# A two-block kernel: the mixers of block 1 with the tensor engine in the order of the plan

## The chip, the cores and the metric

The kernel runs on one NeuronCore of one Trainium2 chip. The metric is the device time of one execution in microseconds (us); less is better. All times below are of executions of the whole program, from its first to its last instruction on that core.

## The reference, cut to what matters

Two blocks follow each other. Block 1 has three mixers on 512 tokens (a gated convolution, a neighbourhood attention, and a gated delta net with 4 heads in two directions), an output projection and a mixture of experts; block 2 comes behind it and isn't touched. Of block 1 the part that matters here is the scan of the delta net: a state is carried from chunk to chunk, and each step needs the state of the one before it.

```python
def _gated_delta_chunked(q, k, v, g, beta):     # once forward, once on flipped inputs
    ...
    sol = lax.linalg.triangular_solve(lower, rhs, left_side=True, lower=True, unit_diagonal=True)
    ...
    def step(state, xs):
        u_c, w_c, intra_c, q_c, k_c, gl_c = xs
        v_new = u_c - jnp.einsum('bhcd,bhde->bhce', w_c, state)
        o_c = jnp.einsum('bhcd,bhde->bhce', q_c, state) + jnp.einsum('bhcs,bhse->bhce', intra_c, v_new)
        state = state * jnp.exp(gl_c)[..., None, None] + jnp.einsum('bhcd,bhce->bhde', k_c, v_new)
        return state, o_c
    _, o = lax.scan(step, s0, xs)
```

The kernel takes chunks of 128 tokens, so a scan has 4 steps.

## The kernel before

The front of block 1 (norm, the first projections, the attention tables) is written in a fixed order. Behind it comes the stage of the change, the **plan**: from about 77 us to about 395 us of the span it runs everything that the mixers need.

The plan (class `Plan`, `run` at L116) is a list of Python generators with priorities. Each `yield cost, delay` tells the plan what the piece just written costs and how long the generator wants to wait before its next piece. `run` takes, at each turn, the first generator by priority whose wait is over. So the order in which instructions are *traced* is made by costs and delays written as constants. Six kinds of generators take part:

- `head(h)` for each of the 4 heads of the delta net: `prep` (decay matrices; a triangular inverse of 16 rows on GpSimd, tiles `Xb`, `Xt`, `XbT`, sent through DRAM by SyncE as `xd` and read back as `X`, `XT`), then `levels` (inverse up to 128 rows: `XT,G`, `X,BT`), then `scan`, then `norm`.
- `kqv` (L714, L737): a convolution's result `cv` or a normalised tile `nat`, transposed by the tensor engine.
- `na_all`: the attention.
- `dense` (lowest priority): the projections `hT,wh` / `hT,wl`, 128x512 matmuls, three per step of 128 input columns, yielded one such step at a time. The weights come as 1 MB tiles `ws` (a pool of 3), are rounded by ScalarE to `wh`, and the rest `wl = ws - wh` is made by VectorE or GpSimd. These matmuls fill the tensor engine's time between the pieces of the heads. `dense` also issues the `adascr` sums of the modulation (VectorE).

The **scan** (L954 to L1018) uses, per step and direction, one PSUM bank `b` in four quarters:

```python
                    mm(q_[0], kq[:, h, c, 0, :], S[d], True, True)             # -> R (DVE)
                mm(q_[1], Y[d][:, c], rhs, True, True)                          # -> vw (ACT)
                    ts_(kd, kn[h][:, c], ekd[:, d, c, h:h + 1], 0.0, OP.mult, OP.add, nc.gpsimd)
                    mm(q_[3], kd, vw, True, True)
                    if step == 0:
                        nc.scalar.copy(Sn, q_[3])                               # L994
                    else:
                        stt(Sn, S[d], egl[:, d, c, h:h + 1], q_[3], OP.mult, OP.add)
                if step:
                    mm(q_[2], kq[:, h, c, 1, :], S[d], True, True)
                mm(q_[0], C["I"][d][:, c], vw, True, True)
```

In the profile `mm` is L186, `stt` L189, `tt` L192, `ts_` L198; the matmul of `q_[3]` is `b<-vw,kd`, that of `q_[2]` is `b<-S,big`, the second one of `q_[0]` is `b<-vw,dec`. A 128x128 matmul in full float32 stands in the trace as two records, a 128x512 one of rounded values as one. Semaphore waits are set between instructions that touch the same tile, and for PSUM the tile is the bank `b`: a matmul into a bank waits for an earlier read of that bank. The read of the new state `Sn` and the matmul into `q_[2]` (at step 0: `q_[0]`) are in one bank.

What each engine then executes is not the traced order. A scheduler of the framework takes the traced instructions and may move them on each engine, as long as data is kept. `in_order` (L210) is the kernel's tool against that: it adds, between one instruction and the next of the engines named, an edge that says "behind this one", without a semaphore. Around the plan it is set for SyncE with `chain=False` (L1107), which keeps the DMA issues of the plan behind those of the front and leaves their order open. The stages behind the plan (output projection, experts, block 2) have their own `in_order` and don't depend on it.

Of the kernel before, what the change touches and what calls it, by code (L numbers as in the profile page):

```python
# [147 lines left out]
def kernel(ctx: ExitStack, tc: tile.TileContext, a: dict, out, dbg=None, stop=99):  # L148
# [56 lines left out]
    def order(i, before):  # L205
        tc.add_manual_dep(i, before.name, mybir.DependencyInfo(mybir.DependencyClass.NoSync, mybir.DependencyReason.DATA),
                          reason="order of issue")

    @contextmanager
    def in_order(chain=True, ENG=ENG):  # L210


        traced = nc.cur_bb.bb.instructions
        last = traced[-1]
        yield
        n = next(k for k in reversed(range(len(traced))) if traced[k] is last) + 1
        prev = {}
        for i in reversed(traced[:n]):
            if i.engine in ENG and i.engine not in prev:
                prev[i.engine] = i  # L220
                if len(prev) == len(ENG):
                    break
        for i in traced[n:]:
            if i.engine in ENG:
                if i.engine in prev:
                    order(i, prev[i.engine])
                if chain:
                    prev[i.engine] = i
# [400 lines left out]
    plan = Plan()  # L629
# [406 lines left out]
    def head(h):  # L1036
        if h > 1:
            yield from need("L%d" % (h - 2))
        yield from prep(h)
        if h > 1:  # L1040
            yield from need("S%d" % (h - 2))
        yield from levels(h)
        yield from scan(h)
        yield from norm(h)
# [12 lines left out]
    def dense():  # L1057
        nat_out()
        for m, (t, x, y) in enumerate(TILES):
            if m < 2:  # L1060
                o = pt0[m]
                if m == 1:
                    nxt_w = slab_tile(2)
            else:
                wl_ = nxt_w
                nxt_w = slab_tile(m + 1) if m + 1 < len(TILES) else None
                o = bank()
                yield from proj_T_steps(o, *wl_, hT, KT)
            plan.done("m%d" % m)
            if m == 2:  # L1070
                zero_scratch()
                decay()
                plan.done("decay", 3.0)
            if m > 2:
                ada_step(1)
            if m > 1:
                ada_load()
            if m == ADX:
                ada_load()
            if m == ADX + 1:  # L1080
                ada_step()
            if m == len(TILES) - 2:
                st["wo"] = wtile(a["w_outT"][0])
            if m == len(TILES) - 1:
                wo_ahead.extend(csplit(st["wo"][:, i], [P, KT, P]) for i in range(2))
            if t == "n":
                post_nqk(x, o)
            elif t == "c":
                post_conv(x, y, o)
            elif t == "z":  # L1090
                zs[x] = ht("zs")
                silu2(zs[x], o, zs[x])
                plan.done("z%d" % x, L_R)
            elif t == "g":
                plan.add(PK, kqv(x, y, o))
        while ada_left or ada_next:
            ada_step()
            ada_load()
        ada_bias(mods2, "bada2", 0, 16)

    def na_all():
        yield from need("m%d" % ORD.rindex("n"))
        yield 0.0, 2.0
        for _ in na_units():
            yield 1.5, L_NA

    with in_order(False, (mybir.EngineType.SP,)):  # L1107
        for h in range(4):
            plan.add(PH[h], head(h))
        plan.add(PN, na_all())  # L1110
        plan.add(PD, dense())
        plan.run()
    f2.close()
    front.close()
    if stop <= 1:
# [1388 lines left out]
```

## Time and profile before

| | |
|---|---|
| time, median of 3 runs (lowest to highest) | 1798.37 us (1794.47 to 1801.24) |
| the profiled execution: its time | 1804.13 us |
| its span, and mean granted clock of the tensor engine | 1802.3 us, 0.951 |
| busy in the span: PE, PEld, DVE, ACT, POOL | 1637.4, 1133.8, 946.3, 641.4, 459.9 us |

PE is TensorE's matmuls, PEld its weight loads, DVE is VectorE, ACT ScalarE, POOL GpSimd, SP SyncE (it issues the DMAs). The tensor engine is busy for 91% of the span. Times in rows are us from the span's start. In a timeline row with "x4" four neighbouring instructions of one kind stand together. A note in square brackets at the end of a row is the idle time of the engine ahead of it and what ended that.

### The profile page before, as it was taken

The page shows a single profiled execution, that of the slowest core. Times are in us where ns is not written, and L with a number is a line of the kernel's source. Part 1 is how long each engine was busy: PE and PEld are TensorE (multiplying, and loading weights), DVE is VectorE, ACT ScalarE, POOL GpSimd, SP SyncE. Part 2 cuts the span into 40 slices and gives each one's busy share as a digit, 9 for nine tenths or more (in the row PEclk, how much of TensorE's full clock was granted, in tenths as well). Part 3 has the DMA queues.
Part 4 walks back from the last instruction along what each step waited for, and adds up shares of the span by engine and source line. Part 5 has one row for each costly group of instructions (what it writes and reads, how often), then busy time and mean ns, then how long its engine had stood idle before and what let it go on. Part 6 is the DMA issues. An engine that isn't in the chain of part 4 may idle for free. (4 is left out here: it accounts for less than half of the span.)

```text
span 1802.3 us, 21878 instructions
## 1 busy us (share of the span) xinstructions
PE 1637.4 (91%) x7938; PEld 1133.8 (63%) x7938; DVE 946.3 (53%) x1832; ACT 641.4 (36%) x1293; POOL 459.9 (26%) x451
## 2 busy tenths in 40 slices
PE   4878989989689989999886889999999899999998
PEld 2767866767333334343332877776888788888886
DVE  6875777773432222222127698665437765335545
ACT  3453563432211100011112646665523554324432
POOL 5364425102100000001110422233115122332251
PEclk7889999999799989999998899999999999999999
DMA  7636244357799999999994574422313232232221
GB/s 282 216 119 201 87 154 154 129 206 293 287 396 421 419 419 421 420 418 418 418 418 175 200 262 160 163 64 78 117 71 129 82 140 88 88 111 100 88 88 47
DMA packets 97213, 385.10 MB, mean 214 GB/s; under 512 B 22624, under 2 KB 46160, under 8 KB 56656
## 3 DMA queue, kind: packets, MB, share of 16 engines
q1 hardware_dynamic: 91120, 371.09, 54.4%
q0 software_dynamic: 5984, 12.59, 1.8%
q8 instruction: 63, 1.03, 0.2%
q14 instruction: 46, 0.38, 0.1%
HBM read 372.61 MB, written 20.47 MB: 218 GB/s over the span
## 5 line engine op out<-in xcount | busy, mean ns | idle before, releaser
L192 POOL TENSOR_TENSOR wl<-ws,wh 128x1024 fp32r<-128x1024 f32 (+1 forms) x60 | 143.4, 2391 | 384.6 <-ACT wh L342 382.4
L186 PE MATMUL b<-ws,xs 128*64 128x512 f32 (+1 forms) x720 | 222.5, 625 | 11.2 <-DMA ws<-in_ew_dram 10.2
L342 ACT CAST wh<-ws 128x1024 fp32r<-128x1024 f32 (+1 forms) x154 | 152.0, 993 | 219.1 <-PE b L186 174.6
L186 PE MATMUL b<-hF,wh 128*128 128x512 f32 x656 | 202.2, 389 | 0.0
L192 DVE TENSOR_TENSOR wl<-ws,wh 128x1024 fp32r<-128x1024 f32 (+1 forms) x94 | 116.2, 1241 | 92.5 <-ACT wh L342 89.4
L186 PE MATMUL b<-hB,wh 128*128 128x512 f32 x512 | 164.3, 401 | 0.0
L189 DVE SCALAR_TENSOR_TENSOR adascr<-ws,crow 128x1024 bf16<-128x1024 f32 x96 | 135.9, 1415 | 8.2 <-DMA ws<-in_wada_dram 7.2
L186 PEld LDWEIGHTS b<-hF,wh 128*128 128x128 f32 x656 | 123.1, 188 | 25.3
L186 PEld LDWEIGHTS b<-ws,xs 128*64 128x64 f32 (+1 forms) x720 | 67.8, 146 | 109.0 <-issue 90.0
L186 PE MATMUL b<-hT,wh 128*128 128x512 f32 x384 | 132.5, 423 | 0.0
L186 PE MATMUL b<-hF,wl 128*128 128x512 f32 x328 | 127.6, 389 | 0.0
L186 PEld LDWEIGHTS b<-hB,wh 128*128 128x128 f32 x512 | 96.3, 191 | 24.7 <-issue 3.2
L189 DVE SCALAR_TENSOR_TENSOR u<-b,cols,u 128x511 f32<-128x511 f32 x88 | 65.8, 748 | 79.6 <-ACT u L2327 78.0
L186 PE MATMUL b<-ws,gT 128*64 128x512 f32 (+1 forms) x376 | 97.6, 607 | 4.3 <-ACT gT L1466 3.6
L192 DVE TENSOR_TENSOR ge<-sil,b 64x512 f32<-64x512 f32 (+1 forms) x32 | 22.1, 690 | 150.6 <-ACT sil L1459 87.1
L186 PE MATMUL b<-hB,wl 128*128 128x512 f32 x256 | 101.1, 395 | 0.0
L186 PE MATMUL b<-wh,gf 128*128 128x512 f32 x288 | 88.6, 389 | 0.0
L186 PE MATMUL b<-hT,wl 128*128 128x512 f32 x192 | 79.5, 414 | 6.7 <-POOL wl L192 4.4
L186 PEld LDWEIGHTS b<-hT,wh 128*128 128x128 f32 x384 | 71.5, 198 | 14.5 <-issue 2.8
L1320 ACT ACTIVATE xs<-b,mods,ab 128x256 f32<-128x256 f32 (+1 forms) x44 | 22.8, 524 | 158.6 <-PE b L186 157.9
L186 PE MATMUL b<-we,xs 128*64 128x512 f32 (+1 forms) x232 | 76.3, 612 | 2.0 <-DMA we<-in_ew_dram 2.0
L186 PEld LDWEIGHTS b<-dg,xg 128*128 128x128 f32 x272 | 39.3, 211 | 60.5 <-issue 57.8
(486 smaller groups left out, 3207.8 us busy)
## 6 DMA issues: line engine op xcount, KB each, us to landing
ws<-in_ew_dram SPq DMA_DIRECT2D x137, 1024.0 KB, 20.8
ws<-in_wada_dram SPq DMA_DIRECT2D x48, 1024.0 KB, 4.9
we<-in_ew_dram SPq DMA_DIRECT2D x40, 1024.0 KB, 20.7
ws<-in_w_upT_dram SPq DMA_DIRECT2D x22, 1024.0 KB, 4.9
ws<-in_w_in2T_dram SPq DMA_DIRECT2D x16, 1024.0 KB, 7.8
kg<-in_ew_dram SPq DMA_DIRECT2D x14, 1024.0 KB, 16.8
ws<-in_w_inT_dram SPq DMA_DIRECT2D x12, 1024.0 KB, 4.9
ws<-in_w_downN_dram SPq DMA_DIRECT2D x8, 1024.0 KB
```

The lines of the kernel that those rows point to most:

```text
L186: nc.tensor.matmul(o, l, r, start=start, stop=stop)
L189: return nc.vector.scalar_tensor_tensor(o, i0, s, i1, op0=op0, op1=op1, **kw)
L192: (eng or nc.vector).tensor_tensor(o, i0, i1, op)
L342: nc.scalar.copy(hi, src)
L1320: nc.scalar.activation(o, b, AF.Identity, scale=A, bias=B)
```

## The change

The plan's run stands in one more context: `in_order(True, (PE,))`. With `chain=True` each instruction of the tensor engine that the plan traces gets an edge behind the one traced before it, so TensorE takes the plan's matmuls strictly in the order in which the plan wrote them. Nothing else is edited; the order on the other engines is still the scheduler's, which now sees other times.

```diff
         plan.add(PN, na_all())
         plan.add(PD, dense())
-        plan.run()
+        with in_order(True, (mybir.EngineType.PE,)):
+            plan.run()
     f2.close()
```

Outside the plan the order of every engine stays as it was (line numbers go up by one). Within it the tensor engine, and through the scheduler the other engines, get another order. Three places:

On the tensor engine, in the scan of head 2, step 1 (`vw,kd` is `q_[3]`, `S,big` is `q_[2]`, `vw,dec` is `q_[0]`; bank `b_2489` is the forward, `b_2493` the backward direction, `b_2449` a projection):

```order
 L186 MATMUL b_2489<-vw_2517,kd_2528 128x128
+L186 MATMUL b_2489<-S_2472,big 128x128
+L186 MATMUL b_2489<-vw_2517,dec_1596 128x128
 L186 MATMUL b_2493<-vw_2520,kd_2537 128x128
+L186 MATMUL b_2493<-S_2479,big 128x128
+L186 MATMUL b_2493<-vw_2520,dec_1694 128x128
 L186 MATMUL b_2449<-hT_116,wh_2132 128x512
 L186 MATMUL b_2449<-hT_117,wh_2132 128x512
-L186 MATMUL b_2489<-S_2472,big 128x128
-L186 MATMUL b_2489<-vw_2517,dec_1596 128x128
-L186 MATMUL b_2493<-S_2479,big 128x128
-L186 MATMUL b_2493<-vw_2520,dec_1694 128x128
```

Before, the other direction's matmul and two projection matmuls stood between the `vw,kd` of a bank and the next matmul into that bank; now nothing does. The plan has 24 such pairs (4 heads, steps 0 to 2, 2 directions), and in the new order the matmul behind `vw,kd` goes into the same bank in all 24; before, 2 to 14 matmuls lay between.

On GpSimd, in the same step of head 2 (`kd` is the factor of the `vw,kd` matmuls above; `Xt`, `Xb` are the row steps of head 3's triangular inverse, `XbT` the copy at its end):

```order
 L192 TENSOR_TENSOR Xb_2312<-Xb_2312,Xt_2313 64x5x11
-L198 TENSOR_SCALAR kd_2528<-nat_1150,ekd 128x128
 L192 TENSOR_TENSOR Xt_2313<-U_2311,Xb_2312 64x48
-L198 TENSOR_SCALAR kd_2537<-nat_1150,ekd 128x128
 L192 TENSOR_TENSOR Xb_2312<-Xb_2312,Xt_2313 64x4x12
 L192 TENSOR_TENSOR Xt_2313<-U_2311,Xb_2312 64x39
```

```order
 L192 TENSOR_TENSOR Xb_2312<-Xb_2312,Xt_2313 64x15
 L901 COPY XbT_2405<-Xb_2312 64x256
+L198 TENSOR_SCALAR kd_2528<-nat_1150,ekd 128x128
+L198 TENSOR_SCALAR kd_2537<-nat_1150,ekd 128x128
 L198 TENSOR_SCALAR kd_2626<-nat_1150,ekd 128x128
 L198 TENSOR_SCALAR kd_2635<-nat_1150,ekd 128x128
```

Both `kd` move from the middle of the row steps to behind the chain and its copy.

On SyncE, where the inverse of head 0 is read back from DRAM (`X`, `XT`, 4 loads) beside the streamed 1 MB weight tiles `ws`:

```order
 L182 DMA ws_1184<-in_wada_dram 128x2048
+L182 DMA ws_1188<-in_w_inT_dram 128x2048
 L915 DMA X_1160<-xd_503 128x4x128
 L915 DMA X_1162<-xd_503 128x4x128
 L915 DMA XT_1164<-xd_504 128x4x128
 L915 DMA XT_1166<-xd_504 128x4x128
-L182 DMA ws_1188<-in_w_inT_dram 128x2048
 L904 DMA xd_505<-Xb_985 64x16x16
```

One weight tile of 1 MB is now issued ahead of the four loads instead of behind them.

## Rows read from the trace of the kernel before

**Rows 1.** Cores: span and mean granted clock.

```profile
core 0: 1802.3 us, clock 0.951
```

**Rows 2.** Windows: from:to length, busy by engine, PEclk, DMA share, GB/s.

```profile
77.00:150.00 73.00, 58.09 (x260) 45.91 (x260) 49.43 (x78) 38.42 (x94) 44.85 (x65) 0.86 0.49 152
150.00:395.00 245.00, 227.28 (x1328) 182.60 (x1327) 180.59 (x363) 113.65 (x279) 76.78 (x123) 0.98 0.44 147
480.00:930.00 450.00, 415.82 (x1912) 165.02 (x1908) 111.81 (x270) 50.06 (x99) 41.25 (x41) 0.96 1.01 415
...
129.90:136.75 6.85, 4.58 (x13) 3.39 (x12) 6.82 (x10) 4.12 (x11) 6.15 (x11) 0.50 0.00 0
```

**Rows 3.** Waits of PE, 60 to 450 us: total, times, longest.

```profile
PE b L714 <- DVE cv L189: 7.9, 4, 2.4
...
PE b L186 <- POOL kd L198: 2.0, 4, 1.2
```

**Rows 4.** Timeline, end of the plan: PE, then SP's expert loads.

```profile
397.41 0.79 PE L186 MATMUL b<-yA,wh 128*128 128x512 f32 x1 [3.52 <-DVE yA L192]
...
411.00 2.34 SPq L182 DMA_DIRECT2D ws<-in_ew_dram  x5
```

**Rows 5.** Timeline, head 0, scan step 1 (start, length, engine, instruction).

```profile
188.38 0.61 PE L186 MATMUL b<-vw,kd 128*128 128x128 f32 x4
...
188.80 0.61 DVE L189 SCALAR_TENSOR_TENSOR S<-S,egl,b 128x128 f32<-128x128 f32 x2 [2.15 <-PE b L186]
188.82 0.49 PE L944 MATMUL b<-ident,X 128*128 128x128 f32 x3
...
189.20 0.49 PE L186 MATMUL b<-S,big 128*128 128x128 f32 x2
```

**Rows 6.** Groups by line and form, 150 to 395 us: reads of the state.

```profile
L189 DVE SCALAR_TENSOR_TENSOR S<-S,egl,b 128x128 f32<-128x128 f32 x16 | 5.0, 341 | 4.7 <-PE b L186 4.7
...
L994 ACT COPY S<-b 128x128 f32<-128x128 f32 x8 | 1.8, 266 | 0.3 <-PE b L186 0.2
```

**Rows 7.** Timeline of POOL, then of PE: `kd` of head 2, step 1.

```profile
291.20 0.36 POOL L198 TENSOR_SCALAR kd<-nat,ekd 128x128 f32<-128x128 f32 x1
...
295.34 0.64 POOL L901 COPY XbT<-Xb 64x256 f32<-64x256 f32 x1
...
291.62 0.49 PE L186 MATMUL b<-vw,kd 128*128 128x128 f32 x2 [0.22 <-POOL kd L198]
```

**Rows 8.** Timeline of SP, then of PE: loads of head 0.

```profile
146.28 1.37 SPq L915 DMA_DIRECT2D XT<-xd  x2
147.71 2.05 SPq L182 DMA_DIRECT2D ws<-in_w_inT_dram  x1
...
152.72 1.13 PE L186 MATMUL b<-XT,G 128*128 128x128 f32 x8 [0.43 <-DMA XT<-xd]
```

**Rows 9.** Timeline of PE, 129 to 145 us: waits of the early stage.

```profile
129.71 0.90 PE L714 MATMUL b<-ident,cv 128*128 128x128 f32 x4 [1.71 <-DVE cv L189]
...
133.31 0.79 PE L186 MATMUL b<-hT,wl 128*128 128x512 f32 x1 [2.27 <-DVE wl L192]
...
144.85 0.79 PE L186 MATMUL b<-hT,wl 128*128 128x512 f32 x1 [4.41 <-POOL wl L192]
```

**Rows 10.** Timeline of PE, head 1: two late inputs and what follows.

```profile
206.50 0.68 PE L186 MATMUL b<-vw,kd 128*128 128x128 f32 x4 [1.86 <-ACT vw L983]
...
220.82 0.49 PE L186 MATMUL b<-vw,kd 128*128 128x128 f32 x2 [1.17 <-POOL kd L198]
...
223.14 1.05 PE L186 MATMUL b<-hT,wh 128*128 128x512 f32 x2
...
227.66 0.63 PE L186 MATMUL b<-hT,wh 128*128 128x512 f32 x2
```

**Rows 11.** Windows behind these two waits (columns as in rows 2).

```profile
222.10:225.50 3.40, 3.40 (x12) 2.90 (x12) 0.41 (x2) 1.73 (x2) 2.63 (x10) 0.50 0.00 0
...
206.50:210.00 3.50, 3.50 (x21) 2.99 (x22) 3.50 (x8) 2.45 (x7) 2.29 (x3) 1.00 0.44 118
```

## The prediction

> **What bounds the kernel now.** I began with the core's span and granted clock [rows 1] and the windows [rows 2]. From 480 to 930 us the DMA engines are full (share 1.01, 415 GB/s); before that stage and behind it the tensor engine (PE) has most of the time. In the plan's stage PE is busy for 227.28 of the 245 us from 150 to 395, while VectorE (DVE) has 180.59, ScalarE 113.65 and GpSimd 76.78: PE sets the pace there, and at most 245 - 227.28 = 17.7 us of its waits could ever be won. From 77 to 150 us it is busy for 58.09 of 73, so waits of other engines weigh more there, up to 14.9 us.
>
> Next the list of PE's waits, and single waits in the timeline [rows 3, 9, 10]: they are few and singly known (the convolution's `cv` 7.9 us in 4 waits, `kd` 2.0 in 4). What the list doesn't show is the scan: its 24 reads of the new state cost PE nothing visible now, since other matmuls stand between.
>
> Last, does a delay in the plan reach the end? Behind the plan's last projection PE waits 3.52 us for `yA` of DVE, then the output projection runs, and the expert weights begin to load at 411.00, behind the routing that follows it [rows 4]. The full DMA stage thus starts later by whatever the plan ends later, and nothing behind it has a fixed clock time. A delay passes one to one, less what that 3.52 us takes up. The span of 1802.3 is 1.8 below the execution's own 1804.13; the median of the runs is 1798.4, so I add the sum to 1804.1 for the profile and to 1798.4 for the forecast.
>
> **The change part by part.**
>
> *The 24 state reads.* Take head 0, step 1 [rows 5]. The four `vw,kd` records begin at 188.38 and the next group at 188.82, so PE spends 0.22 us on one direction. DVE starts the two reads at 188.80; one lasts 0.34 [rows 6], so the first ends at 189.14, and `S,big`, which waits for it through the bank, begins at 189.20. Meanwhile PE did the other direction's `vw,kd` and three `ident,X`. In the new order the matmul into the same bank stands directly behind `vw,kd`: from 188.38 to 189.20 is 0.82 us, of which 0.22 is work, so 0.60 is idle. The plan has 24 such pairs: 24 x 0.60 = **14.4 us**. From below: were only the read itself exposed, 16 x 0.341 (DVE) and 8 x 0.266 (ScalarE) [rows 6] would be 7.6. I take 14.4, since the start-up times are in the same row.
>
> *Reads that come late.* 0.60 holds for a reader that is idle; a single read now holds up everything on PE. DVE is busy 180.59 of 245 us with 363 instructions [rows 2], so a read meets another instruction with chance 0.74, of which on average half of 0.50 us is left: 0.18. For ScalarE, 113.65 of 245 with 279: 0.46 x 0.20 = 0.09. 16 x 0.18 + 8 x 0.09 = **3.6 us**. Bounds: nothing (the reads are moved forward by the scheduler), and a whole instruction each, 16 x 0.50 + 8 x 0.41 = 11.
>
> *`kd` of head 2, step 1.* GpSimd now makes both behind the chain of head 3 and its `XbT` copy. That copy starts at 295.34 and takes 0.64; without the two `kd` in it (0.36 each) it ends at about 295.3, and the first `kd` (0.36) is ready near 295.7, where PE began its `vw,kd` at 291.62 [rows 7]: 4.1 us late. PE itself comes later by the two round trips of step 0, 1.2 us, which GpSimd's chain doesn't wait for. In strict order nothing can be taken ahead of the waiting matmul: projections and every other head stand behind it. **2.9 us**, between 0 (PE already later by more) and 4.1.
>
> *`X` and `XT` of head 0.* Their four loads now stand behind a 1 MB weight tile in SyncE's queue. PE already waits 0.43 for `XT` [rows 8]. 1 MB at the 415 GB/s of [rows 2] is **2.5 us**. Below: 0, if the tile goes out earlier than the loads could have. Above: the tile was issued at 147.71 and `XT` at 146.28 [rows 8]; if the tile waits for a free buffer until then, the issue is late too, by at most 1.4 and its own issue, about 4.3 in all.
>
> *`kd` of head 1, step 2.* These go ahead in GpSimd's order. [...] **-2.8 us**, between 0 and -2.8.
>
> *77 to 150 us.* Here the strict order puts transposes of `cv` and `nat` ahead of projection matmuls that filled time for them, and takes other waits away: DVE's 1.71 (`cv`) and 2.27 (`wl`). But the last wait of the stretch is 4.41 for GpSimd's `wl`, ending at 144.85 [rows 9]. PE may lose or gain some 4.4 us ahead of it and go on at 144.85 all the same. Net **0**: down to -4.4 if GpSimd is earlier, up to about 3 if added waits run past that slack.
>
> *What is taken up again.* Every other engine has the same work as before and more time, so PE finds some of its other inputs ready. Half of the 3.52 for `yA` [rows 4] is 1.8; of the 7.9 for `cv` [rows 3], the longest 2.4 and the 1.71 lie before 150 us, so half of the remaining 3.8 is 1.9. **-3.7 us**, from 0 to -7.3.
>
> *Clock.* One new wait of more than 2 us (`XT`) may bring another stretch at half clock: **+1.6 us**; the new `kd` wait falls in for the one of head 1, whose stretch I took off above, so another **+1.6**. Bounds 0 and six of them, 9.6.
>
> Sum: 14.4 + 3.6 + 2.9 + 2.5 - 2.8 + 0 - 3.7 + 3.2 = 20.1. The terms overlap: PE that is late by one wait meets the next one less late. For that I take off a tenth, to **+18 us**: 1816 as a median, 1822 for a profiled execution.
>
> **The rivals.**
>
> *Absorbed, no change.* PE is only delayed where it bounds. If the delays of the scan used up the idle time that PE has anyway, all 17.7 us of it from 150 to 395 [rows 2] would cover the 18, and the time would be 1798 + 0 to 3, say 1800. For it: most waits there are on engines whose work doesn't grow. Against: much of that idle time lies at places ahead of the scans, and inputs like `cv` are made from PE's own results, which move with it.
>
> *Faster.* From 129.7 to 144.9 PE waits 1.71 + 2.27 + 4.41 = 8.4 us [rows 9]. If in the new order GpSimd makes that `wl` ahead of its chain, all of it goes, and with it the 2.8 of head 1: -11.2. It decides only where the scan costs no more than its reads, 7.6, and other terms nothing: 1798 - 11.2 + 7.6 = 1795; for a measurable gain half the reads must be hidden as well, 1791. For it: these are the longest waits of the stage. Against: GpSimd's order there is set by the chain of head 1, and the new order moves more work in front of it.
>
> *Worse: the pauses bring down the clock.* Each of the 12 scan steps now pauses PE twice by 0.60, 1.2 us in a few microseconds; a single wait of 1.17 came ahead of 3.4 us at half clock, while one of 1.86 at 206.50 was followed by the full clock [rows 10, 11]. If each step cost one such stretch, 12 x 1.6 = 19 would come instead of the 3.2: 1816 + 16 = 1832. Half of the rows speak for it, so one step in several, not each, is what I expect at most. [...]
>
> *The tensor engine reorders for itself*, so that the edges mean little: nothing in the rows shows a matmul that overtook a waiting one; at 206.50 and 220.82 all of PE stood still [rows 10]. [...] I give this rival nothing.
>
> **How the numbers follow.** The forecast, between +9 and +28: 0.63. Absorbed, within 9 us of before: 0.18. Faster by more: 0.07. Worse, +28 and up: 0.12. 0.5% is 9 us, about what a measurement of this kernel can tell from no change: slower 0.63 + 0.12 = 0.75, same 0.18, faster 0.07. The likeliest case's own range is 1807 to 1826. Its low end is the reads alone with `kd` and `XT` (7.6 + 2.9 + 2.5 - 3.7 = 9.3); its high end has the late reads at 11 (20.1 + 7.4 = 27.5). The 80% range reaches down into the absorbed case, to 1800, and up to 1832, the clock's rival; it leaves out faster (0.07), the lower half of the absorbed case (0.07) and the tail above (0.06).
>
> **What would show it.** In the changed profile: each `vw,kd` in the scans followed by a gap of about 0.6 us with DVE `S` or ScalarE `S` as its releaser, a new line in PE's waits of some 14 to 18 us in about 24 waits; PE's busy time from 150 on unchanged, its idle time up by about 18; `vw,kd` of head 2, step 1 waiting 3 us on GpSimd; `XT,G` of head 0 waiting nearly 3 us on a DMA; the first expert load near 411 + 18 = 429; the stage from 480 on the same, only shifted. The prediction fails if the gaps behind `vw,kd` are there but other waits shrink as much, if the expert loads don't shift with the plan, or if DVE's and GpSimd's new orders make inputs late or early in places that I took for equal, above all before 150 us.

## The result and the profile after

| | before | after |
|---|---|---|
| median (lowest to highest) | 1799.28 us (1794.47 to 1801.24, 4 runs) | 1832.51 us (1827.58 to 1833.22, 4 runs) |
| profiled execution: span, mean clock | 1802.3 us, 0.951 | 1830.5 us, 0.951 |

The ratio is 1.0179 with a 95% interval of [1.0164, 1.0194]: the change makes the kernel 32 us slower (1799.3 x 0.0179 = 32.2). The forecast was 18 us slower, 1816, with 1832 as the upper end of its range: the sign is right, the size is about 14 us short. On the forecast's own base it is 1798.4 x 1.0179 = 1830.6, just inside that range. All differences "in us" below are ratios times 1799.3; one ratio is uncertain by about 2 to 4 us, a difference of two by up to 5.

First the windows of the changed kernel, with the columns of [rows 2].

```profile
77.00:150.00 73.00, 52.50 (x239) 41.02 (x237) 46.78 (x75) 35.74 (x90) 40.60 (x56) 0.89 0.43 133
150.00:395.00 245.00, 211.71 (x1216) 172.13 (x1217) 164.03 (x326) 102.17 (x255) 75.36 (x131) 0.95 0.41 137
...
480.00:960.00 480.00, 428.93 (x2003) 176.12 (x2003) 129.10 (x358) 59.19 (x119) 47.76 (x55) 0.95 0.99 403
```

From 150 to 395 us PE is busy for 211.71 us where it was 227.28 [rows 2], and it did 1216 matmul records there instead of 1328: the same work isn't finished by then. The granted clock of that stretch is 0.95 instead of 0.98. From 480 us on the DMA engines are nearly as full as before (share 0.99 against 1.01). Next the list of PE's waits from 60 to 470 us (engine, line, releaser: total, times, longest).

```profile
PE b L186 <- DVE S L189: 12.5, 16, 3.5
PE b L186 <- POOL wl L192: 8.1, 1, 8.1
PE b L714 <- DVE cv L189: 7.5, 4, 2.9
PE b L737 <- DVE nat L192: 5.4, 4, 2.9
PE b L186 <- ACT S L994: 4.0, 8, 1.5
PE b L186 <- DMA XT<-xd: 3.5, 1, 3.5
PE b L186 <- DVE yA L192: 3.3, 2, 2.7
PE b L1027 <- DVE oN L192: 2.8, 2, 1.7
```

Two lines are new, the reads of the state: 16 on DVE and 8 on ScalarE, 16.5 us in all. Before, the list had no such line. GpSimd's `wl` grew from 4.41 [rows 9] to 8.1, `XT` from 0.43 in that place [rows 8] to 3.5. GpSimd's `kd` isn't there any more.

This is the step that [rows 5] show, in the timeline of the changed kernel (head 0, scan step 1):

```profile
197.73 0.39 PE L186 MATMUL b<-vw,kd 128*128 128x128 f32 x2
198.16 0.35 DVE L189 SCALAR_TENSOR_TENSOR S<-S,egl,b 128x128 f32<-128x128 f32 x1 [2.15 <-PE b L186]
...
198.56 0.49 PE L186 MATMUL b<-S,big 128*128 128x128 f32 x2 [0.44 <-DVE S L189]
198.89 0.39 PE L186 MATMUL b<-vw,dec 128*128 128x128 f32 x2
199.11 0.39 PE L186 MATMUL b<-vw,kd 128*128 128x128 f32 x2
...
199.94 0.49 PE L186 MATMUL b<-S,big 128*128 128x128 f32 x2 [0.44 <-DVE S L189]
```

From `vw,kd` to `S,big` it is 0.83 us in both directions (197.73 to 198.56, 199.11 to 199.94), as worked out from before (0.82). The profile calls 0.44 of it idle: it gives `vw,kd` 0.39 us, where PE spent 0.22 on one direction before it went on [rows 5], 0.17 less.

Where the time went, by the start of the same matmul in both traces: +5.5 us at the matmul that waits for GpSimd's `wl` (150.39 against 144.85), +8.0 at head 0's first `XT,G` (160.73 against 152.72), and about +30 at the plan's end. The plan's last wait and the first expert loads moved with it:

```profile
150.39 0.80 PE L186 MATMUL b<-hT,wl 128*128 128x512 f32 x1 [8.09 <-POOL wl L192]
160.73 1.29 PE L186 MATMUL b<-XT,G 128*128 128x128 f32 x8 [3.49 <-DMA XT<-xd]
...
426.87 0.50 PE L186 MATMUL b<-yA,wh 128*128 128x512 f32 x1 [2.69 <-DVE yA L192]
...
442.03 2.57 SPq L182 DMA_DIRECT2D ws<-in_ew_dram  x5
```

The first expert load goes out at 442.03 instead of 411.00 [rows 4], 31 us later. The two profiled spans differ by 28.2 us and the ratio gives 32.2, so within the spread of the runs what the plan loses reaches the end.

Why is GpSimd's `wl` later? These are rows of GpSimd's timeline after: four masks `dec` of head 1, which before stood in the middle of head 0's chain, now stand among its first steps, and the first of them waits for ScalarE.

```profile
113.65 2.50 POOL L192 TENSOR_TENSOR gm<-cm,g 128x512 f32<-128x512 f32 x2
119.47 1.51 POOL L192 TENSOR_TENSOR dec<-dec,cm 128x512 f32<-128x512 f32 x1 [3.32 <-ACT dec L882]
120.94 0.27 POOL L192 TENSOR_TENSOR Xt<-U,Xb 64x15 f32<-64x15 f32 x1
121.17 1.29 POOL L192 TENSOR_TENSOR dec<-dec,qk 128x512 f32<-128x512 f32 x1
...
142.45 0.60 POOL L901 COPY XbT<-Xb 64x256 f32<-64x256 f32 x1
...
148.00 2.33 POOL L192 TENSOR_TENSOR wl<-ws,wh 128x1024 fp32r<-128x1024 f32 x1
```

And the same places before:

```profile
115.10 0.21 POOL L192 TENSOR_TENSOR Xt<-U,Xb 64x15 f32<-64x15 f32 x1 [1.34 <-DMA U<-gd]
...
124.71 1.29 POOL L192 TENSOR_TENSOR dec<-dec,cm 128x512 f32<-128x512 f32 x1
...
136.89 0.63 POOL L901 COPY XbT<-Xb 64x256 f32<-64x256 f32 x1
...
142.46 2.33 POOL L192 TENSOR_TENSOR wl<-ws,wh 128x1024 fp32r<-128x1024 f32 x1
```

The chain begins 5.8 us later (120.94 against 115.10), its copy ends 5.5 later, and `wl` comes 5.5 later. Of the 5.8, the mask ahead of the chain and the wait for its input make 4.8; the rest is a later `gm`, less a shorter wait for the chain's own input.

### The profile page after: what moved, and what is told of

Same layout as the page of the kernel before. It is cut to its first block, busy times and chain, and to the rows that moved or that the text cites. A ratio compares the mean times of both kernels' runs of the same rounds, so it can differ in the third digit from the quotient of the medians.

```text
span 1830.5 us, 21867 instructions
## 1 busy us (share of the span) xinstructions
PE 1641.3 (90%) x7938; PEld 1138.8 (62%) x7938; DVE 949.1 (52%) x1832; ACT 638.7 (35%) x1291; POOL 458.5 (25%) x451
## 4 chain that ended last, share of the span: by engine, by line
PE 47%; DMA 11%; issue 6%; DVE 3%; POOL 2%; ACT 2%; DVEq 0%; POOLq 0%; SPq 0%; ACTq 0%
PE b L186 42%; DMA ws<-in_ew_dram 9%; DMA xg<-ud,gi 2%; PE b L2053 1%; PE b L1877 1%; PE b L1953 1%; DVE big L189 1%; ACT wh L342 1%; POOL wl L192 1%; PE b L2041 1%; PE b L1465 0%; DMA we<-in_ew_dram 0%; PE b L2247 0%; POOL big L192 0%; POOL hF L192 0%
## 5 line engine op out<-in xcount | busy, mean ns | idle before, releaser
L186 PE MATMUL b<-ws,xs 128*64 128x512 f32 (+1 forms) x720 | 223.0, 629 | 12.8 <-DMA ws<-in_ew_dram 12.8
```

The costliest lines, as they stand in the source:

```text
L186: nc.tensor.matmul(o, l, r, start=start, stop=stop)
```

## The experiments

The theory after the result: the strict order costs (a) the unfilled state reads, (b) a later GpSimd chain through the order of the masks, (c) later loads of `X` and `XT`, and (d) a price of its own, since late inputs of any kind are no longer filled. Rivals: the loss is (d) alone, whatever is repaired; or the clock.

| kernel | median us | ratio to before, 95% | us over before |
|---|---|---|---|
| changed | 1832.51 | 1.0179 [1.0164, 1.0194] | 32.2 |
| e1, writes first | 1819.35 | 1.0108 [1.0088, 1.0127] | 19.4 |
| e2, free order, writes first | 1801.07 | 1.0002 [0.9987, 1.0017] | 0.4 |
| e3, strict to the first scan | 1807.45 | 1.0050 [1.0031, 1.0069] | 9.0 |
| e4, strict from the first scan | 1823.11 | 1.0119 [1.0095, 1.0144] | 21.4 |
| e5, masks | 1820.65 | 1.0129 [1.0107, 1.0151] | 23.2 |
| e6, loads | 1828.34 | 1.0158 [1.0137, 1.0180] | 28.4 |
| e7, all three | 1812.90 | 1.0076 [1.0054, 1.0098] | 13.7 |
| e8, free order, masks | 1800.31 | 1.0010 [0.9998, 1.0022] | 1.8 |
| e9, states first | 1818.99 | 1.0104 [1.0086, 1.0121] | 18.7 |
| e10, writes first and masks | 1809.26 | 1.0049 [1.0033, 1.0065] | 8.8 |
| e11, scans free | 1814.35 | 1.0086 [1.0067, 1.0104] | 15.5 |
| e12, strict to the first scan, masks | 1799.53 | 0.9991 [0.9980, 1.0003] | -1.6 |

**e1, e2: the bank's writes ahead of its reads.** In each scan step all matmuls into the bank come first, so none waits for the read of the state. e1 has the strict order, e2 the free one.

```diff
-                    mm(q_[3], kd, vw, True, True)
-                    Sn = ...
                 if step:
                     mm(q_[2], kq[:, h, c, 1, :], S[d], True, True)
                 mm(q_[0], C["I"][d][:, c], vw, True, True)
+                if step < 3:
+                    mm(q_[3], kd, vw, True, True)
+                    Sn = ...
```

> Strict order as in the changed kernel, but each scan step traces its matmuls into the bank in the order q2, q0, q3 and all reads of the bank behind them, so that no matmul waits for the read of the new state. If the 24 state reads are the main price (16.5 us of waits in the changed profile, and their half-clock stretch), the time falls by 15 to 20 us against the changed kernel, to 1812 to 1817, and the waits on S shrink to under 3 us. Rival, any strict order costs the same because the matmuls that filled gaps are fixed elsewhere: within 5 us of the changed kernel, 1827 to 1833, with other waits in their place.

> The kernel before (free order) with the same new order in the scan step. If the scheduler already hid the state reads, there is nothing to win: within 4 us of before, perhaps up to 3 slower since the state is ready 0.44 us later per step. Rival, the reads cost something before too: 5 us or more faster than before.

e1 is 12.8 us under the changed kernel, e2 the same as before. The state reads cost 12.8 us under strict order and nothing under the free one, where other matmuls stood between. That is 2 us short of what was expected of e1: waits of the next step took a part over (PE's waits in e1; the changed kernel has 1.1 for `R`), and head 1's `XT` from DRAM, for which the changed kernel doesn't wait, costs 2.8.

```profile
PE b L186 <- DVE R L189: 3.8, 2, 3.1
PE b L186 <- DVE S L189: 3.1, 2, 2.8
```

The 3.1 for `R` (head 3, step 1) is a read that came late behind other work in DVE's queue (timeline of e1):

```profile
368.01 2.42 POOL L192 TENSOR_TENSOR wl<-ws,wh 128x1024 fp32r<-128x1024 f32 x1
368.17 3.35 DVE L189 SCALAR_TENSOR_TENSOR adascr<-ws,crow 128x1024 bf16<-128x1024 f32 x1
...
372.05 1.21 DVE L189 SCALAR_TENSOR_TENSOR adascr<-ws,crow 128x1024 bf16<-128x1024 f32 x1
...
373.86 0.34 DVE L189 SCALAR_TENSOR_TENSOR R<-b,neg,vn 128x128 f32<-128x128 f32 x1
...
374.25 0.79 PE L186 MATMUL b<-R,X 128*128 128x128 f32 x2 [3.08 <-DVE R L189]
```

**e9: both states first.** Both `vw,kd` and both reads stand ahead of all `q_[2]` and `q_[0]`, in two loops over the directions, so the waits are there but half filled.

```diff
             for (d, c, q_, _), vw in zip(W, V):
                 if step < 3:
                     ...
                     mm(q_[3], kd, vw, True, True)
                     ...
+            for (d, c, q_, _), vw in zip(W, V):
                 if step:
                     mm(q_[2], kq[:, h, c, 1, :], S[d], True, True)
```

> Strict order, with each scan step tracing both directions' vw,kd matmuls first, then both reads, then q2 and q0 of both. Of the 0.82 us between vw,kd and the next matmul into its bank, 0.44 us instead of 0.22 is then filled for the forward direction, and 0.66 for the backward one. If the price is the unfilled part of each round trip, the 24 waits cost 12 x 0.38 + 12 x 0.16 = 6.5 instead of 14.4 us: 8 us under the changed kernel, 1824.5. Rival, the price is the number of waits and not their unfilled length: 1830 to 1834.

The waits fell to about what the unfilled lengths say (6.5), from 16.5 to 5.7 us; 9 of the 24 can still be seen:

```profile
PE b L186 <- DVE S L189: 4.4, 8, 1.7
...
PE b L186 <- ACT S L994: 1.3, 1, 1.3
```

The time fell by 13.5, not 8, as much as with no such wait at all. The waits account for 10.8 of it. Half-clock time explains part of the rest: between 75 and 440 us the granted clock is 0.5 for 37.5 us in e9 and 47.8 in the changed kernel, which is worth some 4.8 (the estimate is in the next section); waits for `R` are 3.5 us longer. So the rival is out: a state read costs by its unfilled part, and where that is filled no wait shows. The expected 8 was too small.

**e3, e4: the strict order in halves.** The edges are made only for the matmuls traced ahead of head 0's scan (e3), or only from there on (e4).

```diff
+            if part:
+                on = on or traced[k_] is st["mark"]
+                if on != (part == "tail"):
+                    continue
             if i.engine in ENG:
```

> Strict order only for the matmuls traced ahead of the first scan, free behind. If the early stage costs what the two traces show at the first common matmuls behind it (GpSimd's wl 5.5 us later, X and XT another 2.5), the time is 1798 + 8 = 1804 to 1808. Rival, early losses are taken up later by idle time: within 3 us of before. Rival, the scans carry nearly all: 1798 to 1801.

> Strict order only from the first scan on, free ahead of it. If the state reads and what follows them carry the rest, 1798 + 20 to 25 = 1818 to 1823. With e3 the two parts should add up to the whole, about 32. Rival, the parts don't add up (an early delay makes the late waits longer): the sum of both is under 25.

9.0 and 21.4: together 30.4 of 32.2, so the parts add up within the noise, and both expectations hold. The early part alone is half the forecast's whole sum, where the prediction had put 0 for this stage and 2.5 for the loads.

**e5, e8: the masks.** One edge puts the four masks of head 1 behind head 1's own chain, in the strict (e5) and in the free order (e8).

```diff
-            tt(x, x, cmb(m), OP.mult, nc.gpsimd)
+            i_ = nc.gpsimd.tensor_tensor(x, x, cmb(m), OP.mult)
+            if h == 1:
+                order(i_.ins, chain_end)
```

> The changed kernel with one edge more: GpSimd's four decay masks of head 1, which had moved in front of head 0's triangular chain, go behind head 1's own chain. If they made the chain end 5.5 us later (142.45 against 136.89 for the copy at its end), PE's wait for GpSimd's wl falls from 8.1 to 3 or less, and the time by 5 to 8 us, to 1825 to 1828. Rival, the chain is late because PE hands it G and dec later: the copy still ends near 143 and the time stays within 3 us of 1832.5.

> The kernel before with only the edge on the masks (behind head 1's chain; before they stood in the middle of head 0's). If GpSimd's chain bounds the stage from 129 to 150 us, head 0's chain ends some 5 us earlier, PE's wait of 4.4 for wl goes, and the time is 3 to 6 us under before, 1795 to 1798. Rival, the gain is eaten by the next late input (cv, XT) or by DVE: the same as before within 2 us.

Under strict order it is worth 9.0 us by the ratio (11.9 by the medians, which later expectations use), a little more than expected. In e5 the chain's copy starts at 130.46 instead of 142.45, and PE waits far less for `wl`, then a little more for `XT`:

```profile
130.46 1.64 POOL L901 COPY XbT<-Xb 64x256 f32<-64x256 f32 x1
...
139.39 0.50 PE L186 MATMUL b<-hT,wl 128*128 128x512 f32 x1 [1.34 <-POOL wl L192]
149.56 2.05 PE L186 MATMUL b<-XT,G 128*128 128x128 f32 x8 [5.07 <-DMA XT<-xd]
```

The matmul at 139.39 is 11.0 us earlier than after the change, and later ones stay 11 to 15 earlier (this profiled execution is the fastest of the four of e5); the time at half clock falls from 47.8 to 27.3 us. In the free order the same edge brings that matmul forward by 4.7 us (140.12 against 144.85), and nothing of it is left: a later tile's rest, DVE's `wl`, is then what PE waits for (e8):

```profile
140.12 0.79 PE L186 MATMUL b<-hT,wl 128*128 128x512 f32 x1 [5.17 <-POOL wl L192]
149.14 1.13 PE L186 MATMUL b<-XT,G 128*128 128x128 f32 x8 [1.37 <-DMA XT<-xd]
160.05 0.80 PE L186 MATMUL b<-hT,wl 128*128 128x512 f32 x1 [4.80 <-DVE wl L192]
```

So moving the masks wins nothing in the kernel before, and the expectation of e8 failed for its rival's reason. They matter where the new order had put them.

**e6: the loads.** One edge puts the 1 MB tile behind head 0's `XT` loads again.

```diff
             st["dma"] = nc.cur_bb.bb.instructions[-1]
+            if "xt0" in st:
+                order(st["dma"], st.pop("xt0"))
```

> The changed kernel with one edge more: the 1 MB weight tile that had moved ahead of the four loads of X and XT of head 0 goes behind them again. If the tile is what they waited for, PE's wait for XT (3.5 us) falls to about 0.5 to 1 and the time by 2.5 us, to about 1830. Rival, the tile is then late itself and PE waits for its rounding: no change, 1832.5.

PE's wait for `XT` falls from 3.49 to 0.61 us, as the edge should do. The time falls by 3.8 us, but the two intervals overlap, so the time alone doesn't show it.

```profile
158.03 1.13 PE L186 MATMUL b<-XT,G 128*128 128x128 f32 x8 [0.61 <-DMA XT<-xd]
```

**e7, e10: together.** e7 has e1, e5 and e6 in one, e10 has e1 and e5.

> Strict order with all three repairs: writes of the bank before its reads, the masks behind the chain, the loads ahead of the tile. If the three are independent and account for the loss, 1832.5 - 13 - 6 - 2.5 = 1811, within 4. What is then left over before, about 11, is the price of strict order itself: late inputs that nothing fills. Rival, the strict order has no price of its own: 1801 or less.

> Strict order with the bank's writes ahead of its reads and the masks of head 1 behind its chain, without the edge on the loads. If the two gains of the single runs (13 and 12) add up, 1832.5 - 25 = 1807.5. Rival, they overlap as in the run with all three: 1813.

e10 is 23.4 us under the changed kernel; 12.8 and 9.0 add up to 21.8. The remaining 8.8 us over before are not taken apart here. In e10 the mask edge brings the matmul that waits for GpSimd's `wl` forward by 7.9 us against e1 (142.69 against 150.62), though PE still waits 6.0 there, for it also gets there earlier: the start of a matmul measures such a gain, the length of its wait doesn't.

```profile
142.69 0.79 PE L186 MATMUL b<-hT,wl 128*128 128x512 f32 x1 [5.95 <-POOL wl L192]
```

e7 is worse than e10 by 4.9, at the edge of the noise. With the tile behind the loads its rest `wl` is late, and PE waits for it, as the rival of e6 said: e7 is 5.3 us ahead of e10 at the first `XT,G` (147.76 against 153.02) and 2.5 behind it at the second (166.19 against 163.73).

```profile
147.76 1.13 PE L186 MATMUL b<-XT,G 128*128 128x128 f32 x8 [2.65 <-DMA XT<-xd]
160.13 0.79 PE L186 MATMUL b<-hT,wl 128*128 128x512 f32 x1 [4.67 <-DVE wl L192]
```

**e11: scans free.** All matmuls traced in the scans carry no edge; the rest of the plan is strict.

```diff
-            if i.engine in ENG:
+            if i.engine in ENG and i.name not in free:
```

> Strict order for all matmuls of the plan but those traced in the scans, which carry no edge of this kind and may go wherever their data allow. If the loss behind 165 us lies in waits inside the scans (state reads, and R, vw and kd that come late with nothing to fill), it goes back to the early part's price: 1798 + 9 = 1807 to 1810. Rival, the strict order of projections and transposes costs by itself there: about 1819, as with the writes moved.

15.5 us over before, between the two expectations: freeing the scans gives back 16.7 of the 32.2. What is left over the early part's 9.0 is 6.5 (itself uncertain by some 5). That this is the price of strict projections and transposes isn't shown: the longest wait of PE behind the early part is now one for a load of head 1 from DRAM, which e3 has too (4.0 us). Before waits 0.5 us at most for it, and the changed kernel not at all.

```profile
250.96 2.08 PE L186 MATMUL b<-XT,G 128*128 128x128 f32 x8 [5.14 <-DMA XT<-xd]
```

**e12: a try for a better kernel.** e3 with the masks of e5.

> Strict order only ahead of the first scan, and the masks of head 1 behind its chain. If the 12 us that the masks were worth under strict order hold here, 1807.5 - 12 = 1795.5, under before by 3 to 4. Rival, as in the free order the gain is eaten by the next late input: 1798 to 1802.

Same as before (-1.6 us, the interval reaches 1.0003). The masks are worth 10.6 against e3, as they are in e10 against e1, but no kernel here beats the one before. With the masks behind the chain, PE's strict order ahead of the first scan costs nothing that can be measured, though PE still waits 3.3 us for `XT` there. So the early part's 9.0 goes with GpSimd's new order, which PE's order brought about, and not with PE's own order as such.

## Why the prediction fell short

- **The 24 state reads, 14.4: right.** The round trip is 0.83 us where 0.82 was read from before. The sum of 14.4 isn't measured by itself: taking the waits away gave 12.8 (e1) and 13.5 (e9), but that takes the late reads of the next term with it (18.0 together) and lets other waits in. The lower bound of 7.6 is excluded, since the shortest waits of the list alone make 9.8.
- **Reads that come late, 3.6: too small.** 24 waits of the shortest kind would be 16 x 0.44 + 8 x 0.35 = 9.8 us of the 16.5 in the list (the profile's idle time, some 0.17 short in each wait); 6.7 is lateness. Two waits make most of it: 3.54 in head 1, step 1, and 1.96 in head 2, step 2. In the first the read stood in DVE's queue behind the `wl` of half a weight tile, which itself waited for a cast (`wh` at 227.75), and that for its DMA (idle for 2.43 us ahead of it):

```profile
226.87 0.39 PE L186 MATMUL b<-vw,kd 128*128 128x128 f32 x2
...
228.82 1.40 DVE L192 TENSOR_TENSOR wl<-ws,wh 128x1024 fp32r<-128x1024 f32 x1 [2.56 <-ACT wh L342]
...
230.41 0.33 DVE L189 SCALAR_TENSOR_TENSOR S<-S,egl,b 128x128 f32<-128x128 f32 x1
230.79 0.50 PEld L186 LDWEIGHTS b<-S,big 128*128 128x128 f32 x2 [3.73 <-DVE S L189]
```

  The estimate took the mean of half an instruction; it had no term for an instruction ahead that is itself waiting.
- **`kd` of head 2, step 1, +2.9: wrong.** PE came there 20 us later than before and GpSimd's chain 15.6 (its step `Xb` 64x28 at 310.04 against 294.46), so the `kd` were ready in time; only 1.2 us of PE's delay had been counted.
- **`X` and `XT`, +2.5: right** in place and in the size of the wait (2.9 us longer, by e6). That it costs as much time isn't shown (3.8 in e6, within the noise, and e12 loses nothing by it). That this tile is needed soon itself was missed (e7).
- **`kd` of head 1, -2.8: half right.** The wait of 1.17 [rows 10] went. No run shows the other 1.6 of this term as the price of a half-clock stretch. What the runs show in its place is that the half clock there stayed: in the changed kernel the granted clock is 0.51 from 229.8 to 236.7, behind the 3.54 above.
- **77 to 150 us, net 0: the step that failed.** The argument was that PE may lose or gain up to 4.4 us and go on with GpSimd's `wl` all the same. It holds only as long as GpSimd's chain keeps its place. The masks that moved in front of it were not priced, and it ended 5.5 us later. e3 measures the stage with the loads at 9.0, and the masks alone are worth 9.0 (e5) to 10.6 (e10, e12). The prediction had named this place as a sign of being wrong: inputs late before 150 us through GpSimd's new order.
- **Taken up again, -3.7: it failed too.** `yA` is 3.3 us in all for 3.52, `cv` 7.5 for 7.9, and `nat` rose from 2.2 to 5.4, `oN` from 0.3 to 2.8. In the free order the gain of the masks is lost at the next late input (e8). In the strict order it is kept (e5: 11 us at 139.39, and still 11 to 15 at the end), but that isn't a rule: e7 loses the gain of its loads at the next late `wl`, in strict order too.
- **Clock, +3.2: a little small.** No run shows the 1.6 that stands in this term twice as the price of one stretch. What the runs show in its place: time at half clock (granted about 0.5), between 75 and 440 us, rose from 37.5 to 47.8 us; in the changed kernel projection matmuls start every 0.43 us there (232.66 to 233.09) against 0.23 at a granted 1.00 (320.47 to 320.70), so by estimate about 10.3 x 0.47 = 4.8 is lost.

The account from PE's side: from 76 us to the output projection (397 before, 428 after) the windows have PE busy for 286.37 of 321 us before and 292.67 of 352 after. So of 31 us, 24.7 are idle time and 6.3 busy time, about 4.5 of that by the clock (the same estimate, in these windows). The idle time by the two lists: state reads +16.5, GpSimd's `wl` +3.7, `XT` +2.6, `nat`, `oN`, a cast `wh` and `gm` together +10.0, all other lines together -8.1 (`kd` -2.0 and DVE's `wl` -1.8 among them).

The rival of the clock came out near this time (1832), but not by its mechanism: it had a half-clock stretch behind each of the 12 scan steps, and two had one (from 229.8 at a granted 0.51, from 325.4 at 0.50). That the time lies inside the range at all is in part luck: the upper end was this rival's, and the likeliest case's own range ended at 1826.

## What to carry to other kernels

Here a strict order cost 32.2 us where inputs weren't ready when an instruction's turn came, and nothing that can be measured ahead of the first scan once the masks stood behind the chain (e12). Look for every place where an engine writes a buffer, another reads it and the next instruction writes it again, count them, and take start to start (here 24 x 0.6 us). Tracing all writes ahead of all reads takes most of that price away without freeing the order (here 12.8 us). And an order fixed on one engine lets the scheduler reorder the others: read the new order of each engine that feeds a wait, since here the stage that was "bound by another engine" lost 9.0 (e5) to 10.6 us (e10, e12) by that engine's own new order.

## What was not expected of the hardware

The same pauses came with either clock. Through head 0's scan PE paused six times (1.49 and 0.82 us, and four of 0.35 to 0.44), and in the changed kernel the granted clock stayed at 1.00; behind the single pause of 3.54 us it was 0.51, as the windows show:

```profile
190.00:208.00 18.00, 14.02 (x107) 12.81 (x107) 8.42 (x22) 8.16 (x23) 4.43 (x8) 1.00 0.24 97
229.80:236.70 6.90, 5.91 (x18) 5.04 (x19) 2.87 (x7) 0.27 (x1) 5.72 (x18) 0.51 0.00 0
```

In e6 the same scan has the same six pauses, and a granted clock of 0.50 follows the first two of them (a row of PE's timeline, then a window):

```profile
188.35 0.49 PE L186 MATMUL b<-vw,dec 128*128 128x128 f32 x2 [1.49 <-ACT S L998]
189.40:192.80 3.40, 3.38 (x16) 3.38 (x17) 0.84 (x2) 0.27 (x1) 2.15 (x3) 0.50 0.60 255
```

e4 is like e6 there (0.50 from 185.5 to 188.9, behind pauses of 1.37 and 0.35), e5 like the changed kernel. So the length of the pauses alone doesn't decide; what does isn't shown here.

A DVE sum `adascr` took 3.35 us beside a GpSimd `wl` (368.17 and 368.01) and 1.21 at 372.05, when that `wl` was over; of the 96 such sums in this trace of e1 it is the longest, and the median is 1.22. That GpSimd's own work made the late `R` of e1 so late is read from this one place and wasn't tried by itself.
